# Gate and up projections as one 2x2x2 block product with seven products, over half-token columns, and FFN pools laid over the attention's

## The chip, the cores and the metric

The kernel runs on one core of a Trainium2 chip. The metric is the device time of one execution in microseconds (us); lower is better. Three executions of the kernel before took 701.97, 702.12 and 705.43 us, median 702.12. A core has TensorE (PE, matrix products into PSUM), VectorE (DVE), ScalarE (ACT), GpSimd (POOL, which works on SBUF only), SyncE (SP, which issues the loads here) and DMA engines. Each engine takes its instructions in order and waits on semaphores for the others.

## The reference

One residual block of an encoder: attention (two groups of heads), a convolutional FFN, and a gated per-layer embedding. 512 tokens, model width 1024, FFN width 2816. The part that matters here:

```
x  = x + concat(mla_heads, diff_heads) @ w_out
h2 = rmsnorm(x) * ffn_norm_g
g  = h2 @ w_gate                      # 1024 -> 2816
c  = conv_b + sum_j shift(g, 2 - j) * conv_w[j]     # causal, width 3
x  = x + (silu(c) * (h2 @ w_up)) @ w_down
x  = x + sigmoid(rmsnorm(x) @ w_pg) * (p @ w_pp)
```

Everything is float32 in the inputs and the output.

## The kernel before

All activations are kept transposed: features on the 128 partitions, the 512 tokens along the free axis. x is eight blocks of [128, 512] (`xb(b)`). A product of float32 numbers is made as three products of rounded halves (`mm3`, lines 151 to 156): each operand is split into hi (rounded by a ScalarE copy, L188 or L147) and lo (the remainder, by a VectorE subtraction, L189, L192 or L148), and PE adds hi*hi, hi*lo and lo*hi into one PSUM bank. The norm's per-token factor is applied after the products, since it commutes with them; the gain of the norm is folded into the split of x.

The FFN runs over f = 0 to 21, each a block of 128 of the 2816 columns (`gu_full`, L782). For each f, `gu_w` loads two weight tiles [128, 8 x 128] from w_gate and w_up and splits them; `gu_mm` makes the gate and the up product, each 8 blocks of the contraction x 3 matmuls with 512 token columns, into a bank each (g, u). `gu_post` (L768) multiplies the gate by the norm's factor nr (VectorE, L772), runs the three-tap convolution (ScalarE L773, VectorE L774 and L775) and silu (ScalarE L776), multiplies by the factor (GpSimd, L777) and by the up bank (VectorE, L778), and splits the result into `ah[f]`, `al[f]`. After every `DOWN_GROUPS` = (6, 6, 6, 4) blocks of f comes the down projection of that group: for each of the eight output blocks b, 3 x nf matmuls of 512 columns (`down`, L794) and an addition to x on VectorE (L575). The halves dh of w_down are loaded as tiles of two f by four b.

Before the FFN, `wo_last` finishes the output projection block by block, each followed by `norm_in` (L736): the split of the block with the gain, its square on ScalarE, and the sum of squares on VectorE or GpSimd (L745). `norm_r` (L747) sums over partitions with a matmul of ones and computes the reciprocal root on tiles of [128, 512]. After the FFN the last down group is followed in the same way by `norm_in` for the embedding stage, which multiplies with w_pg and w_pp (`ple`, L849). Its last block runs as two halves of 256 columns.

The order of PE's instructions is that of the program text; the other engines' queues are ordered by a planner that goes by priorities and its own costs. All tiles lie in one SBUF pool for the whole kernel, with rotating buffers by tag (raw 3, hi and lo 5, th and tl 8, tt 16). PSUM has eight banks: acc 2, lg 3, tp 2, ob 1.

Of the kernel before, what the change touches and what calls it, by code (L numbers as in the profile page):

```python
# [20 lines left out]
P = 128  # L21
T = 512
NT = 4
# [12 lines left out]
# columns of the packed per-partition array  # L36
# [15 lines left out]
DOWN_GROUPS = (6, 6, 6, 4)  # L52
# [3 lines left out]
# units of filling work at the attention's steps  # L56
# [7 lines left out]
# which of VectorE (0) and GpSimdE (1) does a step, by tiles  # L64
# [35 lines left out]
def hybrid_block(ctx: ExitStack, tc: tile.TileContext, a: dict, out: bass.AP):  # L100
# [12 lines left out]
    def tt(name, dtype=F32):  # L113
        return sb.tile([P, T], dtype, tag="tt", bufs=16, name=name)

    def sq_tile(name):
        return sb.tile([P, D], F32, tag="sq", bufs=2, name=name)

    def pm_tile(name):
        return sb.tile([P, T], F32, tag="pm", bufs=PM, name=name)  # L120

    def pt_tile(name):
        return sb.tile([P, T], F32, tag="pt", bufs=2, name=name)

    def xn_tile(name):
        return sb.tile([P, D], F32, tag="xn", bufs=4, name=name)

    def kv_tile(name, dtype=F32):
        return sb.tile([P, NT, H, 160], dtype, tag="kv", name=name)

    def th_tile(name):
        return sb.tile([P, T], F32R, tag="th", bufs=8, name=name), sb.tile([P, T], F32R, tag="tl", bufs=8, name=name + "l")

    def small(name, shape):
        return sb.tile(shape, F32, name=name)

    def load_raw(src, n, name):
        raw = sb.tile([P, 1024], F32, tag="raw", bufs=3, name=f"raw_{name}")
# [3 lines left out]
    def load_w(src, n, name, eng=None):  # L142
        """a tile of weights as hi + lo"""
        raw = load_raw(src, n, name)
        hi = sb.tile([P, 1024], F32R, tag="hi", bufs=NW, name=f"hi_{name}")
        lo = sb.tile([P, 1024], F32R, tag="lo", bufs=NW, name=f"lo_{name}")
# [4 lines left out]
    def mm3(ps, blocks, first=True, last=True):  # L151
        n = len(blocks)
        for i, (xh, xl, wh, wl) in enumerate(blocks):
            TE.matmul(ps, xh, wh, start=first and i == 0, stop=False)  # L154
            TE.matmul(ps, xh, wl, start=False, stop=False)  # L155
            TE.matmul(ps, xl, wh, start=False, stop=last and i == n - 1)  # L156
# [28 lines left out]
    def split(h_, l_, src, col=None, eng=None):  # L185
        """hi and lo of src, times a gain for each partition"""
# [9 lines left out]
    # the tensor engine's clock and the activation tables get ready while the first loads run  # L196
    ones, warm = small("ones", [P, P]), small("warm", [P, 1])
# [11 lines left out]
    def squares(kq):  # L209
        """squares of x, for the sums over its columns"""  # L210
# [7 lines left out]
    cols = small("cols", [P, NCOL])  # L218
    nc.sync.dma_start(cols, a["cols"])
    xh, xl, wa = [], [], []  # L220
    for kq in range(4):
        raw = xn_tile(f"xT{kq}")
        xraw.append(raw)
        wr = sb.tile([P, 1024], F32, tag="raw", bufs=3, name=f"raw_a{kq}")
        wh, wl = (sb.tile([P, 1024], F32R, tag=i, bufs=NW, name=f"{i}_a{kq}") for i in ("hi", "lo"))
# [21 lines left out]
    ident = small("ident", [P, P])  # L247
# [20 lines left out]
    # latents: normalise  # L268
# [19 lines left out]
    # weights of the up-projections  # L288
# [64 lines left out]
    st_ = sb.tile([P, NK, T], F32R, tag="st", name="st")  # L353
# [11 lines left out]
    # rope tables with the gains folded in: [c g1 | c g2], [-s g2 | s g1]  # L365
# [16 lines left out]
    # rope of the shared key  # L382
# [11 lines left out]
    # gains of the MLA heads: those of k's nope part go to q's side, with the scale  # L394
# [3 lines left out]
    # differential heads: both gains and minus the scale on q's side  # L398
# [55 lines left out]
    # -lambda on every partition  # L454
# [21 lines left out]
    def probs_T(pm, t, name, on_act):  # L476
        """transposed probabilities of a tile of queries"""
# [59 lines left out]
    def bias_strip():  # L537
        """minus the relative position bias as a strip for each head, S[p, h, j] = -f_h(j - 384 - p)"""
# [9 lines left out]
        strip = sb.tile([P, DH, T], F32, tag="strip", name="strip")  # L548
# [16 lines left out]
    def wo_blocks(k0, k1, b, w):  # L565
        """blocks k0..k1 of the contraction of w_out with the mixer's output, for a block of x^T"""
# [3 lines left out]
    def xb(b):  # L570
        """a block of x^T"""
# [10 lines left out]
    def wo_units(kq, dqs, nk):  # L582
        """the product with the first nk blocks of a half of w_out's rows, added to x^T"""
# [366 lines left out]
```

## Time and profile before

| | |
|---|---|
| Median of three runs | 702.12 us |
| Profiled execution | span 706.7 us; no other time is given for it |
| PE busy | 677.1 us, 3242 matmuls |
| VectorE busy | 424.2 us, 754 instructions |
| ScalarE busy | 288.4 us |
| GpSimd busy | 139.0 us |
| DMA | 63.38 MB, mean 90 GB/s |

Engines overlap, so the busy times do not add up to the span. A matmul's row shows its latency, with an end that is modelled; the rate is read from the distance between starts. A row of instructions gives the start, the duration, the engine, the line, the operation, the output tile and its inputs, and in brackets how long the engine had been idle and what released it. Line numbers are those of the kernel before.

### The profile page before, as it was taken

The numbers are of one execution on the slowest core, as the hardware profiler recorded it, in microseconds if no ns is written. First come the engines' busy times: TensorE is split into PE (matmuls) and PEld (weight loads), VectorE is DVE, ScalarE is ACT, GpSimd is POOL, SyncE is SP. The second block draws the span as 40 slices with busy tenths as digits, with TensorE's granted clock in tenths as the row PEclk, the third lists the DMA queues.
The fourth block names the chain that finished last, engine by engine and source line by source line (L and its number), as shares of the span: only waits on it lengthen the run. The fifth ranks groups of instructions, "written<-read, shape, count | busy, mean of one in ns | idle before, by whom it ended". The sixth has DMA issues, their size and how long they took to land.

```text
span 706.7 us, 8596 instructions
## 1 busy us (share of the span) xinstructions
PE 677.1 (96%) x3242; PEld 554.8 (79%) x3242; DVE 424.2 (60%) x754; ACT 288.4 (41%) x500; POOL 139.0 (20%) x136
## 2 busy tenths in 40 slices
PE   7988889999999997999999999999999999999997
PEld 6877678788878785788888888888888888877886
DVE  6689964634779878774544545534554455468743
ACT  6156645536666654343421333312333233255210
POOL 6458341504010125021100011100101000132000
PEclk9899999999999998999999999999999999999999
DMA  7332014303311103233213333222233132243101
GB/s 261 106 121 89 30 60 135 120 1 111 129 30 61 31 31 105 74 99 110 90 42 108 119 102 106 90 90 89 90 103 103 63 119 90 89 150 104 60 31 45
DMA packets 19552, 63.38 MB, mean 90 GB/s; under 512 B 2220, under 2 KB 2988, under 8 KB 19384
## 3 DMA queue, kind: packets, MB, share of 16 engines
q1 hardware_dynamic: 18776, 60.25, 25.9%
q0 software_dynamic: 448, 2.37, 1.1%
q8 instruction: 25, 0.41, 0.2%
q10 hardware_dynamic: 288, 0.23, 0.1%
q14 instruction: 15, 0.12, 0.1%
HBM read 60.73 MB, written 3.42 MB: 91 GB/s over the span
## 4 chain that ended last, share of the span: by engine, by line
PE 76%; DVE 14%; ACT 3%; issue 2%; POOL 2%; DMA 2%; SPq 0%; ACTq 0%; DVEq 0%; POOLq 0%
PE u L154 6%; PE u L156 6%; PE u L155 6%; PE g L156 6%; PE g L155 6%; PE g L154 6%; PE dn L154 5%; PE dn L155 5%; PE dn L156 5%; PE pg L154 2%; PE pg L156 2%; PE pg L155 2%; PE mo L527 2%; PE zd L154 2%; PE zd L156 2%
## 5 line engine op out<-in xcount | busy, mean ns | idle before, releaser
L777 POOL TENSOR_TENSOR cv<-cv,nr 128x512 f32<-128x512 f32 x22 | 28.7, 1308 | 297.9 <-ACT cv L776 297.9
L155 PE MATMUL g<-h2l,hi_g 128*128 128x512 f32 x176 | 69.6, 396 | 4.7 <-DVE h2l L192 4.7
L154 PE MATMUL dn<-ah,hi_dn 128*128 128x512 f32 x176 | 69.8, 397 | 2.1 <-DVE x L575 2.1
L154 PE MATMUL u<-h2h,hi_u 128*128 128x512 f32 x176 | 70.5, 401 | 0.0
L154 PE MATMUL g<-h2h,hi_g 128*128 128x512 f32 x176 | 70.4, 400 | 0.0
L156 PE MATMUL u<-h2h,lo_u 128*128 128x512 f32 x176 | 70.2, 399 | 0.0
L156 PE MATMUL g<-h2h,lo_g 128*128 128x512 f32 x176 | 70.0, 398 | 0.0
L155 PE MATMUL u<-h2l,hi_u 128*128 128x512 f32 x176 | 69.6, 396 | 0.0
L156 PE MATMUL dn<-ah,lo_dn 128*128 128x512 f32 x176 | 69.5, 395 | 0.0
L575 DVE TENSOR_TENSOR x<-x,dn 128x512 f32<-128x512 f32 x32 | 21.9, 685 | 51.1 <-PE dn L156 51.1
L147 ACT CAST hi_dn<-raw_dn 128x1024 fp32r<-128x1024 f32 x22 | 23.1, 1051 | 69.3 <-PE dn L155 29.7
L772 DVE TENSOR_TENSOR gr<-g,nr 128x512 f32<-128x512 f32 x22 | 15.1, 691 | 53.7 <-PE g L156 53.6
L147 ACT CAST hi_g<-raw_g 128x1024 fp32r<-128x1024 f32 x22 | 23.0, 1047 | 57.9 <-PE dn L155 39.9
L147 ACT CAST hi_u<-raw_u 128x1024 fp32r<-128x1024 f32 x22 | 23.1, 1052 | 55.4 <-PE g L155 50.0
L155 PEld LDWEIGHTS g<-h2l,hi_g 128*128 128x128 f32 x176 | 33.3, 189 | 13.9 <-DVE h2l L192 5.9
L778 DVE TENSOR_TENSOR cv<-cv,u 128x512 f32<-128x512 f32 x22 | 15.1, 688 | 44.4 <-POOL cv L777 44.4
L154 PEld LDWEIGHTS dn<-ah,hi_dn 128*128 128x128 f32 x176 | 33.0, 187 | 10.8 <-DVE x L575 1.9
L154 PE MATMUL zd<-hi_d,xh 128*128 128x512 f32 x96 | 40.2, 418 | 0.0
L156 PEld LDWEIGHTS u<-h2h,lo_u 128*128 128x128 f32 x176 | 33.5, 190 | 8.4
L155 PEld LDWEIGHTS u<-h2l,hi_u 128*128 128x128 f32 x176 | 33.5, 190 | 8.2
L156 PEld LDWEIGHTS g<-h2h,lo_g 128*128 128x128 f32 x176 | 33.3, 189 | 8.1
L154 PEld LDWEIGHTS u<-h2h,hi_u 128*128 128x128 f32 x176 | 33.6, 191 | 7.7
(371 smaller groups left out, 1657.4 us busy)
## 6 DMA issues: line engine op xcount, KB each, us to landing
raw_g<-in_w_gate SPq DMA_DIRECT2D x22, 512.0 KB, 3.6
raw_u<-in_w_up SPq DMA_DIRECT2D x22, 512.0 KB, 3.5
raw_dn<-in_w_down SPq DMA_DIRECT2D x22, 512.0 KB, 3.5
raw_d<-in_w_d SPq DMA_DIRECT2D x12, 512.0 KB, 3.7
raw_o<-in_w_out SPq DMA_DIRECT2D x8, 512.0 KB, 4.0
raw_pg<-in_w_pg SPq DMA_DIRECT2D x8, 512.0 KB, 3.6
x<-in_xT SPq DMA_DIRECT2D x4, 512.0 KB, 5.6
out<-ot SPq DMA_DIRECT2D x7, 256.0 KB, 2.0
```

Source lines behind the costliest of these rows:

```text
L147: S.copy(hi[:, :n], raw[:, :n])
L154: TE.matmul(ps, xh, wh, start=first and i == 0, stop=False)
L155: TE.matmul(ps, xh, wl, start=False, stop=False)
L156: TE.matmul(ps, xl, wh, start=False, stop=last and i == n - 1)
L527: TE.matmul(po[:, w], pt[:, tsl[j]], kv[j][:, h, 96:], start=j == 0, stop=j == t)
L575: V.tensor_tensor(xb(b), xb(b), ps, op=ALU.add)
L772: V.tensor_tensor(gr, pg_, nrm["r"], op=ALU.mult)
L777: G.tensor_tensor(cv, cv, nrm["r"], op=ALU.mult)
L778: V.tensor_tensor(cv, cv, pu, op=ALU.mult)
```

## The change

Gate and up of one f are written as one product of 2x2 blocks: the weights' two halves of the contraction by (gate, up), and x's two halves of the contraction by the two halves of the tokens (256 columns each). Four quadrants of the result (gate and up, first and second half of the tokens) come from seven products, each of 4 contraction blocks x 3 matmuls with 256 columns, in place of the eight of plain blocks. Operands of these products are sums and differences of quadrants.

- `w_prep(f)` loads the two weight tiles, forms the four weight sums (two on GpSimd, two on VectorE, 512 wide each) and splits four tiles (three of 1024, one of 512) into hi and lo.
- `tokens(k)`, for k = 0 to 3, forms from x blocks k and k + 4 the token quadrants and four sums on GpSimd (256 wide each), and splits them.
- `gu_units(f)` is a generator of seven units. PSUM banks are used again without clearing: x collects P1, then P1 + S2 T2, then also S3 T3; y collects S1 T1, then also S4 b22. ScalarE copies x out three times, VectorE combines to the four quadrants.
- `gu_post` multiplies gate and up by the norm's factor in one VectorE operation of 1024; the GpSimd multiplication is gone.
- `norm_r` sums squares to [128, 4] with tokens on the partitions, takes the root there, and `norm_b` spreads the factor with a diagonal matrix and a matmul of ones. All square sums are on VectorE.
- `DOWN_GROUPS` is (4, 4, 4, 4, 6). The down products of the first four groups are units of a filling queue, two of them in each f from 5 to 20; the last group follows f = 21.
- The last blocks of the output projection run in the order 0, 4, 1, 5, 2, 6, 3, 7.
- There are pools of their own for attention (`att`, `wts`), FFN (`ffn`, `dwn`) and embedding (`ple`), a later one laid over an earlier one, where a new tile waits for the old tiles that it lies over. Raw weight tiles have 4 buffers in the FFN, hi and lo of the down weights 2.

```
-DOWN_GROUPS = (6, 6, 6, 4)
+DOWN_GROUPS = (4, 4, 4, 4, 6)
...
-    sb = ctx.enter_context(tc.tile_pool(name="sb", bufs=1))
+    keep = ctx.enter_context(tc.tile_pool(name="keep", bufs=1))
+    att = tc.alloc_tile_pool(name="att", bufs=1, side="left")
+    wts = tc.alloc_tile_pool(name="wts", bufs=1, side="right")
...
+    order = (0, 4, 1, 5, 2, 6, 3, 7)
...
+    att.release()
+    wts.release()
+    ffn = tc.alloc_tile_pool(name="ffn", bufs=1, side="left", reuse_waits="tile")
+    dwn = tc.alloc_tile_pool(name="dwn", bufs=1, side="right", reuse_waits="tile")
+    wp.update(pool=dwn, rawpool=ffn, raw=4, w=2)
...
+    def w_prep(f):
+        ra, rb = (load_raw(a[w][f], 1024, f"{w[2]}{f}") for w in ("w_gate", "w_up"))
+        sa, sb = (ffn.tile([P, 1024], F32, tag=i, name=f"{i}{f}") for i in ("sa", "sb"))
+        l, r = slice(0, 512), slice(512, 1024)
+        G.tensor_tensor(sa[:, r], rb[:, l], rb[:, r], op=ALU.add)
+        V.tensor_tensor(sa[:, l], sa[:, r], ra[:, l], op=ALU.subtract)
+        G.tensor_tensor(sb[:, l], ra[:, l], rb[:, l], op=ALU.subtract)
+        V.tensor_tensor(sb[:, r], ra[:, r], sa[:, l], op=ALU.subtract)
+        w = {}
+        for i, (src, n, keys) in enumerate(((ra, 1024, ("11", "12")), (sa, 1024, ("S2", "S1")), (sb, 1024, ("S3", "S4")), (rb[:, r], 512, ("22",)))):
+            h_, l_ = (ffn.tile([P, n], F32R, tag=f"{j}{i}", bufs=2 if i == 0 else 1, name=f"{j}{i}_{f}") for j in ("wh", "wl"))
+            split(h_, l_, src)
...
+    def tokens(k):
+        gu = ffn.tile([P, 2, T], F32, tag="gu", bufs=2, name="xg")
+        for j in range(2):
+            S.activation(gu[:, j], xb(k + K2 * j), AF.Identity, scale=cols[:, C_FFN + k + K2 * j:C_FFN + k + K2 * j + 1])
+        split(b11[0][:, k], b11[1][:, k], gu[:, 0, t1])
+        split(b2[0][:, k], b2[1][:, k], gu[:, 1])
+        ts_ = ffn.tile([P, 4, H2], F32, tag="s", bufs=2, name="ts")
+        G.tensor_tensor(ts_[:, 0], gu[:, 0, t2], gu[:, 0, t1], op=ALU.subtract)
+        G.tensor_tensor(ts_[:, 1], gu[:, 1, t2], ts_[:, 0], op=ALU.subtract)
+        G.tensor_tensor(ts_[:, 2], gu[:, 1, t2], gu[:, 0, t2], op=ALU.subtract)
+        G.tensor_tensor(ts_[:, 3], ts_[:, 1], gu[:, 1, t1], op=ALU.subtract)
+        split(bt[0][:, k], bt[1][:, k], ts_)
...
+    def product(ps, w, b, more=False):
+        mm3(ps, [(w[0][:, tsl_k[k]], w[1][:, tsl_k[k]], b[0][:, k], b[1][:, k]) for k in range(K2)], not more, True, more)
...
+    def gu_units(f, w):
+        x = bank("acc", f"gx{f}")[:, :H2]
...
+        product(x, w["11"], tb["11"])
+        S.copy(s[:, 0], x)
+        yield
+        p2 = bank("tp", f"ga{f}")[:, :H2]
+        product(p2, w["12"], tb["21"])
+        V.tensor_tensor(gu[:, 0, t1], s[:, 0], p2, op=ALU.add)
+        yield
+        product(x, w["S2"], tb[2], True)
+        S.copy(s[:, 1], x)
+        yield
+        y = bank("lg", f"gb{f}")[:, :H2]
+        product(y, w["S1"], tb[1])
+        yield
+        p4 = bank("tp", f"gc{f}")[:, :H2]
+        product(p4, w["22"], tb[4])
+        yield
+        product(x, w["S3"], tb[3], True)
+        S.copy(s[:, 2], x)
+        V.tensor_tensor(gu[:, 1, t1], s[:, 2], p4, op=ALU.subtract)
+        V.tensor_tensor(gu[:, 1, t2], s[:, 2], y, op=ALU.add)
+        yield
+        product(y, w["S4"], tb["22"], True)
+        V.tensor_tensor(gu[:, 0, t2], s[:, 1], y, op=ALU.add)
+        gu_post(f, gu)
+        yield
...
     def gu_post(f, gu):
...
-        V.tensor_tensor(gr, pg_, nrm["r"], op=ALU.mult)
+        V.tensor_tensor(gu, gu, nrm["r"].unsqueeze(1).broadcast_to([P, 2, T]), op=ALU.mult)
...
-        G.tensor_tensor(cv, cv, nrm["r"], op=ALU.mult)
-        V.tensor_tensor(cv, cv, pu, op=ALU.mult)
+        V.tensor_tensor(cv, cv, up, op=ALU.mult)
...
+    w = {0: w_prep(0)}
+    for k in range(K2):
+        tokens(k)
+        for b in (k, k + K2):
+            square(b, dwn)
+    g = gu_units(0, w[0])
+    next(g)
+    next(g)
+    for f in range(NF):
+        if f + 1 < NF:
+            w[f + 1] = w_prep(f + 1)
+            g1 = gu_units(f + 1, w[f + 1])
+        if f == 0:
+            next(g1)
+            next(g1)
+            norm_r()
+            next(g)
+            norm_b(ffn)
+        else:
+            next(g)
+        for _ in range(3):
+            next(g)
+        if f and f + 1 < NF:
+            next(g1)
+        if f:
+            pump()
+        for _ in g:
+            pass
+        if f and f + 1 < NF:
+            next(g1)
+            pump()
+        for f0, nf in groups[:-1]:
+            if f == f0 + nf:
+                fill.append(down_units(f0, nf))
+        g = g1
+    pump(100)
```

So within one f from 1 on, PE's order is: products S2, S1, 22, S3 of f, product 11 of f + 1, a down unit, product S4 of f, product 12 of f + 1, a down unit.

More of the change, by code (lines that the diff above doesn't have):

```diff
@@ L741, in norm_in, with square @@
+    def square(b, pool):
+        if "ss" not in nrm:
+            nrm["ss"] = pool.tile([P, T], F32, tag="ah", bufs=8, name="ss")
             S.activation(nrm["ss"], xb(b), AF.Square)
         else:
-            sq = pt_tile("nsq")
+            sq = pool.tile([P, T], F32, tag="al", bufs=8, name="nsq")
             S.activation(sq, xb(b), AF.Square)
-            (G if b % 2 else V).tensor_tensor(nrm["ss"], nrm["ss"], sq, op=ALU.add)
+            V.tensor_tensor(nrm["ss"], nrm["ss"], sq, op=ALU.add)
@@ L747, in norm_r @@
     def norm_r():
-        ps = bank("ob", "nr")
-        TE.matmul(ps, ones, nrm["ss"], start=True, stop=True)
-        r, m, g, t = (w_[:, i] for w_ in [sb.tile([P, DH, T], F32, tag="strip", name="nr")] for i in range(4))
-        rms(r, ps, T, D, m, (g, t))
-        return r
-    h2h = sb.tile([P, NK, T], F32R, tag="st", name="h2h")
-    h2l = kv_tile("h2l", F32R).rearrange("p t h d -> p (t h d)")[:, :NK * T].rearrange("p (k t) -> p k t", t=T)
+        ss, ps = nrm.pop("ss"), bank("ob", "nr")
@@ new lines, in hybrid_block, with load_w3, norm_in @@
+    pump(100)
+    ffn.release()
+    ple_ = tc.alloc_tile_pool(name="ple", bufs=1, side="left", reuse_waits="tile")
+    def load_w3(src, name):
+        raw = ple_.tile([P, 1024], F32, tag="raw", bufs=3, name=f"raw_{name}")
+        nc.sync.dma_start(raw, src)
+        h_, l_ = (ple_.tile([P, 1024], F32R, tag=i, bufs=NW, name=f"{i}_{name}") for i in ("hi", "lo"))
+        split(h_, l_, raw)
+        return h_, l_
+    def norm_in(b, hh, hl_, c):
+        split(hh[:, b], hl_[:, b], xb(b), cols[:, c + b:c + b + 1])
+        square(b, dwn)
@@ L874, in hybrid_block @@
     ple(NK - 1, w, 256, 512)
+    ple_.release()
+    dwn.release()
 def _constants():
```

172 lines of the change are left out of this document (88 added, 84 removed).

## The prediction

> **What bounds the kernel now.** I read the page's busy shares first, then the busy time by stage, then single instructions of the stage that the change rebuilds.
>
> ```profile
> span 706.7 us, 8596 instructions
> PE 677.1 (96%) x3242; PEld 554.8 (79%) x3242; DVE 424.2 (60%) x754; ACT 288.4 (41%) x500; POOL 139.0 (20%) x136
> ```
>
> ```profile
> 257.00:285.00 28.00, 23.33 (x89) 18.16 (x88) 22.71 (x21) 14.69 (x22) 14.32 (x7) 0.88 0.29 94
> 285.00:360.00 75.00, 75.00 (x323) 60.16 (x322) 46.90 (x60) 28.34 (x35) 9.33 (x7) 1.00 0.30 92
> 360.00:640.00 280.00, 277.94 (x1194) 223.56 (x1192) 137.82 (x160) 89.64 (x110) 28.29 (x21) 1.00 0.30 98
> ```
>
> The columns of the second view are the stretch, PE, PE weight loads, VectorE, ScalarE, GpSimd, granted clock, DMA. TensorE (PE) is the bound: in the FFN's 360 to 640 us it is busy 277.94 of 280, at full clock, while VectorE works 137.82, about half. Only the entry of the FFN, 257 to 285, is not PE's: there VectorE is busy 22.71 of 28 and the granted clock falls to 0.88. Busy PE time hides overlap, so I take the step from one matmul to the next:
>
> ```profile
> 330.42 0.40 PE L154 MATMUL g<-h2h,hi_g 128*128 128x512 f32 x1
> ...
> 335.77 0.40 PE L156 MATMUL g<-h2h,lo_g 128*128 128x512 f32 x1
> ```
>
> ```profile
> 698.83 0.29 PE L154 MATMUL pg<-h3h,hi_pg 128*128 128x256 f32 x1
> ...
> 701.54 0.28 PE L156 MATMUL pg<-h3h,lo_pg 128*128 128x256 f32 x1
> 701.55 0.19 PEld L154 LDWEIGHTS pp<-pt,pp 128*128 128x128 f32 x1
> ```
>
> The first pair brackets 24 matmuls of 512 columns: 5.35/23 = 0.2326 us each. The second brackets 24 of 256 columns, each with a weight load of its own: 2.71/23 = 0.1178 us. So half the columns cost half the time.
>
> **TensorE's part of the change.** Gate and up for one f (128 FFN columns) were 2 x 8 x 3 = 48 matmuls of 512: 48 x 0.2326 = 11.16 us. Seven products of 4 x 3 matmuls of 256 are 84 x 0.1178 = 9.90. That removes 1.27 us per f, 27.9 us over 22. The down projection keeps its 528 matmuls (24 x 0.2326 = 5.58 us per f), in groups (4,4,4,4,6): of the first four, 32 units of 12 matmuls, two in each of f = 5 to 20; the last group grows from 8 x 12 to 8 x 18 matmuls.
>
> [...] The 0.1178 us step, with a load in every step, says the load is hidden; the measured step decides.
>
> **VectorE's part.** Its prices, from back-to-back rows:
>
> ```profile
> 405.22 0.75 DVE L774 SCALAR_TENSOR_TENSOR cv<-gr,cols,cv 128x511 f32<-128x511 f32 x1
> 406.00 0.75 DVE L775 SCALAR_TENSOR_TENSOR cv<-gr,cols,cv 128x510 f32<-128x510 f32 x1
> ...
> 409.66 1.23 DVE L148 TENSOR_TENSOR lo_g<-raw_g,hi_g 128x1024 fp32r<-128x1024 f32 x1
> 410.80 0.69 DVE L189 TENSOR_TENSOR al<-cv,ah 128x512 fp32r<-128x512 f32 x1
> ...
> 606.82 0.69 DVE L189 TENSOR_TENSOR pt0l<-raw_p,pt 128x512 fp32r<-128x512 f32 x1
> 607.42 0.69 DVE L189 TENSOR_TENSOR pt1l<-raw_p,pt 128x512 fp32r<-128x512 f32 x1
> ...
> 698.32 0.42 DVE L862 TENSOR_TENSOR sg<-pg,nr 128x256 f32<-128x256 f32 x1 [1.35 <-PE pg L156]
> ```
>
> A 1024-wide operation occupies 1.14 us, a 512-wide one 0.60, a scalar_tensor_tensor 0.78; a 256-wide one lasts 0.42, less the same 0.09 of overlap 0.33. Per f the new kernel has on VectorE: two of the weights' sums, 1.20; low halves of three 1024-wide and one 512-wide tile, 4.02; four 256-wide combinations of PSUM, 1.32; the post step (1024-wide multiply by the norm, two scalar_tensor_tensors, two 512-wide) 3.90. Together 10.44. From f = 5 on, a down weight (1.14) and two adds to x (1.20) make it 12.78. The old kernel's list at the same prices (three 1024-wide, three 512-wide, two scalar_tensor_tensors, 8/6 of an add) is 7.6 us beside 16.7 of PE. New: 10.44 beside 9.90 for f = 0 to 4, and 12.78 beside 15.48 later.
>
> **GpSimd's part, and what it does to VectorE.** Per f GpSimd gives up one 512-wide multiply and gets two 512-wide sums:
>
> ```profile
> L777 POOL TENSOR_TENSOR cv<-cv,nr 128x512 f32<-128x512 f32 x22 | 28.7, 1308 | 297.9 <-ACT cv L776 297.9
> L426 POOL TENSOR_TENSOR qn<-rt 128x256 f32<-128x256 f32 x4 | 3.0, 747 | 3.3 <-DVE rs_t L172 2.6 <-DVE rt L425 0.3 <-POOL rt L423 0.3
> ```
>
> That is 2.6 us per f. The old multiply ran while VectorE waited for it anyway; the new sums run beside a loaded VectorE. What that costs shows in the old FFN's entry (two views, VectorE and GpSimd):
>
> ```profile
> 267.58 2.89 DVE L745 TENSOR_TENSOR ss<-ss,nsq 128x512 f32<-128x512 f32 x1
> 270.40 0.67 DVE L575 TENSOR_TENSOR x<-x,o 128x512 f32<-128x512 f32 x1
> ...
> 272.95 2.26 DVE L192 SCALAR_TENSOR_TENSOR h2l<-x,cols,h2h 128x512 fp32r<-128x512 f32 x1
> ```
>
> ```profile
> 267.07 2.85 POOL L148 TENSOR_TENSOR lo_g<-raw_g,hi_g 128x1024 fp32r<-128x1024 f32 x1
> 270.62 1.26 POOL L745 TENSOR_TENSOR ss<-ss,nsq 128x512 f32<-128x512 f32 x1 [0.69 <-DVE ss L745]
> 271.84 2.83 POOL L148 TENSOR_TENSOR lo_u<-raw_u,hi_u 128x1024 fp32r<-128x1024 f32 x1
> ```
>
> VectorE's 0.69 us add took 2.89 and ended at 270.47, 0.55 after GpSimd's operation ended at 269.92; the scalar_tensor_tensor took 2.26 and ended 0.54 after GpSimd's. A VectorE operation with two SBUF inputs waits the GpSimd operation out. The add to x, with one input in PSUM, took 0.67 under GpSimd as always. So GpSimd's time is added to VectorE's wherever it meets two-SBUF work: 9.12 of the 10.44 us (87%), which gives 10.44 + 0.87 x 2.6 = 12.7 for f = 0 to 4; later 10.26 us of such work in a 15.48 us period (66%), 12.78 + 1.7 = 14.5. The ends are 10.4 and 13.0, 12.8 and 15.4. I take 12.5 for f = 0 to 4: VectorE is the bound there by 2.6 us per f. For f = 5 to 20 it is loaded to 94% of PE's period, in a queue kept in order, with operations that wait for ScalarE and PE; I take 16.0 us, between PE's 15.48 and 17.0 (12.78 + 2.6 + some 1.6 of waits, two STT prices).
>
> **The entry of the FFN.** The old one lost this on PE:
>
> ```profile
> 272.49 0.51 PE L155 MATMUL g<-h2l,hi_g 128*128 128x512 f32 x1 [2.85 <-DVE h2l L192]
> ...
> 275.27 0.80 PE L155 MATMUL g<-h2l,hi_g 128*128 128x512 f32 x1 [1.82 <-DVE h2l L192]
> 275.86 0.63 PE L156 MATMUL g<-h2h,lo_g 128*128 128x512 f32 x1
> ...
> 281.41 0.41 PE L154 MATMUL u<-h2h,hi_u 128*128 128x512 f32 x1
> ```
>
> Idle 4.67, and 13 steps at 0.427 instead of 0.2326, 2.5: 7.2 us. The new kernel first makes the token operands, for each of four pairs of blocks: on VectorE splits of 256, 512 and 1024 (0.33 + 0.60 + 1.14) and two square sums (1.20; the squares that GpSimd added are VectorE's now), 3.27; on GpSimd four 256-wide sums at 0.75, 3.0. Times four, 13.1 + 12.0 = 25.1, nearly all of it two-SBUF work, so one after the other. The two engines also prepare weights for f = 0 (5.22 + 2.6); their raw tiles lie over attention tiles that the last head's norm still reads shortly before the entry, so I put half of that, 3.9, behind.
>
> ```profile
> 257.12 2.73 DVE L575 TENSOR_TENSOR x<-x,o 128x512 f32<-128x512 f32 x4 [1.27 <-PE o L156]
> ```
>
> The adds to x start at 257.12 and take 0.68; after the first pair of them and two 512-wide gains on ScalarE, token work starts near 260. Operands of all seven products are ready at 260 + 25.1 + 3.9, some 288 (282 if weights are early and GpSimd's sums slip under the adds; 293 with all weights behind). PE meanwhile has four products for f = 0 and 1, 5.65 us, and then waits. Reordering the output projection keeps its matmuls; its adds to x merely arrive in pairs. The norm's four-wide rsqrt replaces 512-wide steps, which PE's queue hid; with its diagonal it costs VectorE about as much as the part of f = 1's weights that fits in the waits saves: nothing.
>
> **New waits.** S4 adds onto the bank of S1, so PE waits for one ScalarE copy and two VectorE steps after S3, all 256-wide; behind it queue the next f's product and a down unit. For f above 4 a product and a unit of 2.8 us lie between: hidden. At f = 21 nothing does: 1.3 us (three steps of 0.42) to 1.7 with the signals between. ScalarE was busy 89.64 of 280 us, 5.4 per f; even with twice that it would not be the bound. Down weights have two buffers: casts for the next half wait for the last unit, with five products (7.1 us) as cover and 2.3 us of VectorE work in it; that is in the 16.0. DMA counts are unchanged (66 FFN tiles of 512 KB).
>
> The last group now follows f = 21 at once; before, four units of 18 matmuls lay between. Its weights lie over token operands that S4 reads last: a load (3.5, the row below), cast, low half (1.14) come after it, while f = 21's post step ends; the first 12 matmuls cover 2.8. I take 6 us, bounds 3 and 9.
>
> ```profile
> raw_dn<-in_w_down SPq DMA_DIRECT2D x22, 512.0 KB, 3.5
> ```
>
> The embedding stage's first matmul follows its last one:
>
> ```profile
> 645.70 0.40 PE L154 MATMUL pg<-h3h,hi_pg 128*128 128x512 f32 x1
> ```
>
> **The sum**, in the profile's time: 288 + 5 x 12.5 - 3.9 (the post step of f = 4 runs under f = 5) = 346.6; + 16 x 16.0 = 602.6; f = 21, five products and the stall, 7.1 + 1.7 = 611.4; + 6 = 617.4; + 144 x 0.2326 = 650.9; the embedding stage as before, 706.7 - 645.7 = 61.0: 711.9. That is 5.2 above the old span of 706.7. The span is the only time shown for that execution; it lies 4.6 above the runs' median of 702.12 and 1.3 above the highest run, so I carry the difference over: **707 us**. The 27.9 us saved on PE go: some 10 at the entry, some 12 in f = 0 to 4, 8 in f = 5 to 20, 4 at the tail beyond what was lost there before.
>
> **Rivals.** *VectorE keeps up.* GpSimd's sums fall into VectorE's waits and under PSUM operations: operands at 284, 11.0 per f, then PE's own 15.48, a 4 us tail: 284 + 55 - 3.9 + 247.7 + 8.8 + 4 + 33.5 + 61 = 690, 17 less than before: 686 us. For it: the demand, 14.5, is under 15.48, and most dependences have several microseconds of slack. Against: f = 0 to 4 stay above PE even at 10.44. It decides if VectorE's share in f = 5 to 20 stays under about 95% with PE dense.
>
> *VectorE is the bound all along.* At 17.0 us per f from f = 5 on, 16 more: 723 us. For it: 15.4 without any overlap, plus waits for activations in a fixed order; against: the schedule has other work to put in.
>
> *Weight loads show.* If a 256-column step cost a load's 0.188 us (its row above, 0.19), PE would need 15.8 per f, 22 x 4.6 = 102 more than before, about 804. The 0.1178 steps speak against it; what is new is only that they go on for long.
>
> **Chances.** Forecast 0.46 (699 to 717), VectorE keeps up 0.33 (679 to 698), VectorE bound 0.19 (717 to 735), weight loads 0.02. Half a per cent, 3.5 us, is what this measurement tells from no change. Of the forecast's 0.46, 0.18 lie within it and 0.28 above. So faster 0.33, same 0.18, slower 0.28 + 0.19 + 0.02 = 0.49. All low ends together give 679, all high ends 734; I take 682 to 727.
>
> **What would show it.** The 256-column step: 0.118, else the fourth case. VectorE's busy share above 95% for f = 1 to 4 and PE idle there some 2.5 us per f, released by VectorE; VectorE rows of 1.2 us stretched past 2 where GpSimd runs. PE's period for f = 5 to 20: 15.5 means the first rival, 17 the second. First S2 product near 288; an idle of some 6 us on PE before the last group. I am wrong if PE is dense from 300 on, or if the operands are ready before 280.

## The result, and the profile after

The changed kernel takes 737.83 us (median of 4 runs, 735.52 to 740.57) beside 703.7 for the kernel before in the same comparison: ratio 1.0482, 95% interval 1.0437 to 1.0527. It is 4.8% slower; the prediction was 707, with a range of 682 to 727. The page of the changed kernel, and its busy time by stage in the columns of the prediction's second view:

```profile
span 738.8 us, 10590 instructions
PE 665.8 (90%) x4050; PEld 589.0 (80%) x4050; DVE 549.0 (74%) x956; ACT 351.6 (48%) x624; POOL 178.2 (24%) x162
```

```profile
257.00:285.00 28.00, 10.38 (x40) 7.61 (x38) 22.80 (x22) 14.44 (x23) 17.63 (x14) 0.72 0.11 38
285.00:360.00 75.00, 54.82 (x381) 52.27 (x382) 57.33 (x84) 35.32 (x53) 18.48 (x15) 0.85 0.19 57
360.00:640.00 280.00, 266.91 (x1858) 250.04 (x1856) 236.79 (x316) 131.31 (x195) 54.15 (x33) 0.98 0.30 93
```

TensorE worked 23.33 of 28 us and all of the next 75 before; now 10.38 and 54.82, at granted clocks of 0.72 and 0.85. In the last row PE is short by 13 us, most of it at the end. So PE lacks work at the entry, less so up to f=5, and at the tail, and not in between.

**The entry.** ScalarE, TensorE, VectorE and GpSimd rows of the changed kernel:

```profile
264.27 1.33 ACT L780 ACTIVATE xg<-x,cols 128x512 f32<-128x512 f32 x2 [9.38 <-PE o L160]
```

```profile
293.34 0.58 PE L160 MATMUL gx<-b11l,wh 128*128 128x256 f32 x1 [2.31 <-DVE b11l L194]
...
298.88 0.38 PE L161 MATMUL gx<-b11h,wl 128*128 128x256 f32 x1 [1.64 <-DVE wl L194]
...
303.93 0.36 PE L159 MATMUL gx<-bth,wh 128*128 128x256 f32 x1
```

```profile
276.46 1.21 DVE L798 TENSOR_TENSOR ss<-ss,nsq 128x512 f32<-128x512 f32 x1
...
295.55 1.21 DVE L194 TENSOR_TENSOR btl<-ts,bth 128x1024 fp32r<-128x1024 f32 x1
```

```profile
275.95 1.17 POOL L787 TENSOR_TENSOR ts<-ts,xg 128x256 f32<-128x256 f32 x1
...
278.88 2.18 POOL L759 TENSOR_TENSOR sa<-raw_u 128x512 f32<-128x512 f32 x1 [1.76 <-DVE wl L194]
```

ScalarE sat 9.38 us before the first token operand and was released by an output-projection matmul, though the adds to x had begun at 256.96. Then VectorE and GpSimd work against each other until GpSimd ends at 293.87: the 512-wide VectorE operation shown takes 1.21 (0.69 alone), a 256-wide GpSimd one 1.17 (0.75 alone), a 512-wide one 2.18 (1.31). The last VectorE row is the last token operand, ready at 296.76; at 1024 columns 1.21 is its ordinary duration. TensorE finishes the first product at 293.9, waits again for f=1's weights, and begins S2 of f=0 at 303.93.

**f=1 to 4.** S4 of f=0 and of f=4 on TensorE, 51.7 us apart, 12.9 per f; then that stretch by engines, and what VectorE and, from 300 to 372, TensorE waited for (us in total, times, longest):

```profile
315.78 0.39 PE L159 MATMUL gb<-b2h,wh 128*128 128x256 f32 x1 [2.51 <-DVE gu L851]
...
367.49 0.39 PE L159 MATMUL gb<-b2h,wh 128*128 128x256 f32 x1 [2.19 <-DVE gu L851]
```

```profile
315.50:367.50 52.00, 42.77 (x325) 41.96 (x325) 43.09 (x58) 27.47 (x41) 13.03 (x8) 0.93 0.25 76
```

```profile
DVE gu L854 <- PE gb L161: 5.5, 4, 2.0
DVE sa L760 <- POOL sa L759: 2.2, 3, 1.2
```

```profile
PE gb L159 <- DVE gu L851: 11.5, 5, 2.5
```

VectorE is busy 83%, not full: it waits for S4 (gu L854 needs bank gb) and for GpSimd's sum, while TensorE waits for VectorE before S4. They wait in turn. For TensorE the period of 12.9 is 84 steps of 0.120 (10.1), 2.2 of wait and some 0.6 of slower steps: its granted clock in that stretch is 0.93, and 0.52 from 316.90 to 320.40, behind the first of these waits.

**f=5 to 20, and the tail.** The middle of the FFN, then S4 of f=21, the last group, and ScalarE's queue between them:

```profile
375.00:623.00 248.00, 246.62 (x1707) 230.37 (x1706) 213.58 (x285) 116.75 (x171) 49.31 (x30) 1.00 0.31 94
```

```profile
622.85 0.28 PE L159 MATMUL gx<-bth,wh 128*128 128x256 f32 x1
...
623.81 0.28 PE L161 MATMUL gx<-bth,wl 128*128 128x256 f32 x1
...
630.02 0.39 PE L159 MATMUL gb<-b2h,wh 128*128 128x256 f32 x1 [1.25 <-DVE gu L851]
...
639.99 0.80 PE L159 MATMUL dn<-ah,hi_dn 128*128 128x512 f32 x1 [8.28 <-ACT hi_dn L193]
...
642.27 0.63 PE L160 MATMUL dn<-al,hi_dn 128*128 128x512 f32 x1
642.70 0.63 PE L161 MATMUL dn<-ah,lo_dn 128*128 128x512 f32 x1
```

```profile
633.47 0.81 ACT L864 ACTIVATE cv<-gu,cols 128x512 f32<-128x512 f32 x1 [4.29 <-DVE gu L863]
...
638.90 1.99 ACT L193 CAST hi_dn<-raw_dn 128x1024 fp32r<-128x1024 f32 x2
```

In the middle PE is dense (246.62 of 248) at full clock with VectorE at 86%, and a 256-column matmul with its weight load takes 0.96/8 = 0.120 us. Behind S4 of f=21 nothing covers its post step: the cast of the last group's weights stands behind the activations of f=21 in ScalarE's queue, PE idles 8.28 us and starts the last group with steps of 0.43 us, about twice the usual (granted clock 0.53 from 640 to 645).

### The profile page after: what moved, and what is told of

Same layout as the page of the kernel before. It is cut to its first block, busy times and chain, and to the rows that moved or that the text cites. A ratio compares the mean times of both kernels' runs of the same rounds, so it can differ in the third digit from the quotient of the medians.

```text
span 738.8 us, 10590 instructions
## 1 busy us (share of the span) xinstructions
PE 665.8 (90%) x4050; PEld 589.0 (80%) x4050; DVE 549.0 (74%) x956; ACT 351.6 (48%) x624; POOL 178.2 (24%) x162
## 4 chain that ended last, share of the span: by engine, by line
PE 59%; DVE 20%; issue 8%; POOL 5%; ACT 4%; DMA 3%; SPq 0%; POOLq 0%; ACTq 0%; DVEq 0%
PE dn L161 5%; PE dn L159 5%; PE dn L160 5%; PE gx L159 3%; PE gx L160 3%; PE gx L161 3%; DVE wl L194 2%; PE gb L159 2%; PE gb L161 2%; PE gb L160 2%; PE mo L532 2%; PE pg L161 2%; PE pg L160 2%; PE pg L159 2%; PE zd L159 2%
## 5 line engine op out<-in xcount | busy, mean ns | idle before, releaser
L759 POOL TENSOR_TENSOR sa<-raw_u 128x512 f32<-128x512 f32 x22 | 39.7, 1805 | 140.8 <-DMA raw_u<-in_w_up 65.2
L160 PE MATMUL dn<-al,hi_dn 128*128 128x512 f32 x176 | 69.6, 396 | 0.0
L761 POOL TENSOR_TENSOR sb<-raw_g,raw_u 128x512 f32<-128x512 f32 x22 | 33.6, 1528 | 110.1 <-DVE wl L194 110.1
L159 PE MATMUL gx<-bth,wh 128*128 128x256 f32 x176 | 50.6, 287 | 0.7 <-ACT s L840 0.6
L160 PE MATMUL gx<-btl,wh 128*128 128x256 f32 x176 | 50.3, 286 | 0.0
L161 PE MATMUL gx<-bth,wl 128*128 128x256 f32 x176 | 50.3, 286 | 0.0
L160 PE MATMUL zd<-lo_d,xh 128*128 128x512 f32 x96 | 38.1, 396 | 0.0
L159 PEld LDWEIGHTS gx<-bth,wh 128*128 128x128 f32 x176 | 34.2, 195 | 1.8 <-ACT s L840 1.1
L160 PEld LDWEIGHTS gx<-btl,wh 128*128 128x128 f32 x176 | 34.3, 195 | 0.7
L161 PEld LDWEIGHTS gx<-bth,wl 128*128 128x128 f32 x176 | 34.3, 195 | 0.0
## 6 DMA issues: line engine op xcount, KB each, us to landing
out<-ot SPq DMA_DIRECT2D x7, 256.0 KB, 2.0
```

Source lines behind the costliest of these rows:

```text
L159: TE.matmul(ps, xh, wh, start=first and i == 0, stop=False, skip_group_check=again)
L160: TE.matmul(ps, xh, wl, start=False, stop=False, skip_group_check=again)
L161: TE.matmul(ps, xl, wh, start=False, stop=last and i == n - 1, skip_group_check=again)
L759: G.tensor_tensor(sa[:, r], rb[:, l], rb[:, r], op=ALU.add)
L761: G.tensor_tensor(sb[:, l], ra[:, l], rb[:, l], op=ALU.subtract)
```

## Experiments

All ratios are to the kernel before, run on the same chip; the changed kernel's is 1.0482. Savings in us are differences of such ratios times 704. In profiled executions the FFN's beginning differs by 1 to 3 us, so stages are compared from a row near it.

**Where the first scratch lies.**

```diff
+    early_t = {0: (ffn.tile([P, 2, T], F32, tag="gu", bufs=2, name="xg"), ffn.tile([P, 4, H2], F32, tag="s", bufs=2, name="ts"))}
     b11, b2, bt = hl("b11", [P, K2, H2]), hl("b2", [P, K2, T]), hl("bt", [P, K2, 4, H2])
...
-        gu = ffn.tile([P, 2, T], F32, tag="gu", bufs=2, name="xg")
+        gu, ts_ = early_t.pop(k) if k in early_t else (ffn.tile([P, 2, T], F32, tag="gu", bufs=2, name="xg"), None)
```

> Only the place of the scratch of the first token pair is changed: xg and its sums lie over attention tiles that are free early, not over the w_out weights that the last output-projection matmul reads. If the place of the scratch is what delays the entry, ScalarE's first xg row comes before 260 us and no longer behind an o matmul, the product S2 of f=0 starts near 298 instead of 303.9, and the time falls by about 6 us, to some 732. If the 25 us of serial VectorE and GpSimd work sets the entry by itself, whatever it waits for at the start, the start moves by as much all the same: 4 to 6 us. If the weights of f=0 set the end of the entry (the product 11 waits for b11 of the last pair, which stands behind them in ScalarE's and VectorE's queues), the first xg comes earlier and S2 does not: under 2 us.

735.5 us, ratio 1.0414 (1.0377 to 1.0452). ScalarE's first row there:

```profile
254.66 1.40 ACT L781 ACTIVATE xg<-x,cols 128x512 f32<-128x512 f32 x2 [2.80 <-DVE x L580]
```

The wait for the o matmul is gone, xg follows x at once. S2 of f=0 came at 296.16; with 3.0 us by which this execution was early already at ScalarE's last yh row (251.16 against 254.20), that is 4.7 earlier. The ratios differ by 0.0068, 4.8 us. Their intervals just overlap (1.0437 against 1.0452), but the profile shows the same 4.7: the place of the scratch costs about 5 us.

**GpSimd's sums on VectorE.** All six lines of this kind:

```diff
-        G.tensor_tensor(sa[:, r], rb[:, l], rb[:, r], op=ALU.add)
+        V.tensor_tensor(sa[:, r], rb[:, l], rb[:, r], op=ALU.add)
```

> All sums that GpSimd made (two per f of the weights, four per pair of the tokens) are on VectorE instead; the results are the same. By the lock (a VectorE operation with two SBUF inputs waits out a GpSimd operation) GpSimd's time is VectorE's time already, at GpSimd's dearer price (0.75 against about 0.33 us for 256 columns, 1.3 against 0.6 for 512): the entry's 25.1 us become 13.1 + 16 x 0.33 = 18.4, S2 of f=0 comes some 6 us earlier, f=1 to 4 cost at most what they did (12.9 us each), and the time falls by 5 to 9 us. By the rival, that GpSimd really works beside VectorE, VectorE gets 1.2 us more per f and 5.3 us more at the entry: f=1 to 4 take about 14 us each, f=5 to 20 rise from 15.7 to above 16, and the time rises by 5 us or more.

727.69 us, ratio 1.0306 (1.0276 to 1.0336): 12.4 us less, more than either end of the expectation. VectorE in f=1 to 4, and its two convolution lines (us in total, mean ns), here and then in the changed kernel:

```profile
310.00:356.00 46.00, 41.31 (x336) 40.50 (x337) 44.57 (x66) 28.58 (x41) 0.00 (x0) 1.00 0.32 100
```

```profile
L865 DVE SCALAR_TENSOR_TENSOR cv<-gu,cols,cv 128x511 f32<-128x511 f32 x22 | 16.4, 748 | 0.9 <-ACT cv L864 0.9
L866 DVE SCALAR_TENSOR_TENSOR cv<-gu,cols,cv 128x510 f32<-128x510 f32 x22 | 16.4, 744 | 0.0
```

```profile
L865 DVE SCALAR_TENSOR_TENSOR cv<-gu,cols,cv 128x511 f32<-128x511 f32 x22 | 25.6, 1164 | 1.9 <-ACT cv L864 1.7
L866 DVE SCALAR_TENSOR_TENSOR cv<-gu,cols,cv 128x510 f32<-128x510 f32 x22 | 22.7, 1030 | 0.0
...
L760 DVE TENSOR_TENSOR sa<-sa,raw_g 128x512 f32<-128x512 f32 x20 | 13.8, 692 | 21.4 <-POOL sa L759 21.4
```

VectorE did 60 operations more and its busy time rose by only 5.1 us (549.0 to 554.1): 44 of 0.60 and 16 of 0.33 are 31.7 us, so some 27 us of stretch went, and 21.4 us of waiting for GpSimd's sum besides. Stretch and waiting together were more than the 31.7 us of the work itself. Now VectorE is full in f=1 to 4, 97%. S4 of f=0 and of f=4 begin at

```profile
309.86 0.39 PE L159 MATMUL gb<-b2h,wh 128*128 128x256 f32 x1 [1.25 <-DVE gu L851]
...
354.46 0.39 PE L159 MATMUL gb<-b2h,wh 128*128 128x256 f32 x1 [1.28 <-DVE gu L851]
```

That is 11.15 us per f, and 11.6 in the last two of the four; 10.44 plus the two sums at 0.60 is 11.64. How the two engines meet shows in the changed kernel's trace: GpSimd's 512-wide sum at 269.77 lasted 2.28 (1.31 alone), to 272.05, beside a VectorE split that ended at 270.92, and the next VectorE split, 1024 wide, at 270.84, lasted 2.29 (1.21 alone), to 273.13. So each ended 1.1 us after the one before it on the other engine.

**S4 later.**

```diff
+            next(g1)
             for _ in g:    # S4 of f
                 pass
-            next(g1)
```

> Only the order on TensorE changes, for f=1 to 20: the second product of f+1 (12) runs before S4 of f instead of behind it, which puts 2.8 us instead of 1.4 between S3 and S4 where there is no down unit. If f=1 to 4 are slow because S4 waits for a chain of short steps on ScalarE and VectorE (2.0 to 2.5 us of TensorE idle each), they fall from 12.9 to 11 to 11.5 us and the total by 5 to 8 us. If VectorE's throughput with GpSimd's locks is the bound there, as predicted, the wait appears elsewhere: 12.5 us or more each, total within 2 us. For f=5 to 20 no change either way.

734.71 us, ratio 1.0402 (1.0378 to 1.0426), 5.6 less. What VectorE waited for in this kernel's f=1 to 4:

```profile
314.00:364.40 50.40, 42.75 (x336) 41.94 (x336) 45.80 (x56) 26.53 (x40) 13.35 (x8) 0.97 0.28 84
```

```profile
DVE gu L854 <- PE gb L161: 2.6, 2, 1.8
DVE sa L760 <- POOL sa L759: 1.2, 1, 1.2
```

Neither theory: the period fell only to 12.6, PE still waited about 2 us before most S4, and VectorE's share rose from 83 to 91%. VectorE's wait for S4 was one part of the loop; with it shortened VectorE is nearer its limit. Between S2 of f=0 and S2 of f=5 the trace accounts for 3 of the 5.6 us (65.0 against 68.0); some 1.5 lie ahead of S2 of f=0, where nothing was changed.

**The seven products undone.**

```diff
-        product(x, w["11"], tb["11"])
...
+        product(pg_, w["11"], b1)
...
+        product(pg_, w["12"], b2, True)
...
```

Six more of the seven products go, and the bank of up, pu, gets the same two lines.

> The changed kernel without the seven products: gate and up as four plain block products of 512 columns (48 matmuls), no sums of weights or tokens, no combinations; the pools over the attention's, the four-wide norm, the order of the f and the down groups (4,4,4,4,6) stay; the result is the same function. If the seven products (their operands, combinations and locks) cost the time, this goes to between 698 and 712: TensorE needs 11.16 us per f where it took 12.9 in f=1 to 4, and 16.7 per f for f=5 to 20 against 15.7 (16 us worse), while the entry is at least 15 us shorter. If the pools, the norm and the new tail cost it, it stays above 725, with f=0 to 4 at 11.2 and the entry and tail as late as in the changed kernel.

707.58 us, ratio 1.0025 (1.0003 to 1.0047). So pools, norm and groups cost 0.25%, the seven products, with the operands that they need, the other 4.6. Up's first product of f=8 and that of f=10 begin there, and product 22 of f=12 and f=14 in the changed kernel, at

```profile
383.44 0.39 PE L159 MATMUL gb<-b1h,wh 128*128 128x512 f32 x1
...
416.34 0.39 PE L159 MATMUL gb<-b1h,wh 128*128 128x512 f32 x1
```

```profile
484.55 0.28 PE L159 MATMUL gc<-bth,wh 128*128 128x256 f32 x1
...
515.64 0.28 PE L159 MATMUL gc<-bth,wh 128*128 128x256 f32 x1
```

That is 32.90/2 = 16.45 us per f against 31.09/2 = 15.55: where PE is dense, the seven products gain 0.90 us per f. In f=1 to 4, without down units, it is the other way round: there the plain kernel takes 10.88 us per f (the same product begins at 290.58 for f=1 and at 334.10 for f=5) where the changed one takes 12.9.

**The tail's cover.**

```diff
-DOWN_GROUPS = (4, 4, 4, 4, 6)
+DOWN_GROUPS = (2, 4, 4, 4, 4, 4)
```

> Only the down projection's groups change: (2, 4, 4, 4, 4, 4) instead of (4, 4, 4, 4, 6), so that four units of 12 matmuls are left when f=21 is reached, one between its S3 and S4 and three (8.4 us) behind S4, and the last group has 12 matmuls per block instead of 18. If the gap before the last group is want of cover, the 8.28 us and the steps at half clock behind it (some 2.5 us) go, f=3 and 4 pay 1 to 2 us each for adds that come earlier, and the time falls by 8 to 10 us, to some 729. If the last group's weights themselves come late (they lie over token operands that S4 of f=21 reads), the gap stays at 3 to 5 us behind the three units and the time falls by 4 us or less.

728.24 us, ratio 1.0330 (1.0300 to 1.0359), 10.7 less. TensorE behind f=21 in that kernel:

```profile
636.23 0.50 PE L159 MATMUL dn<-ah,hi_dn 128*128 128x512 f32 x1 [0.59 <-ACT hi_dn L193]
...
638.76 0.50 PE L161 MATMUL dn<-ah,lo_dn 128*128 128x512 f32 x1 [1.80 <-DVE lo_dn L194]
```

The 8.28 became 0.59 and 1.80, though some eight steps of 0.43 remain: want of cover, as the first theory had it. Not all of the saving lies there. S4 of f=21 began at 625.88 instead of 630.02, though a unit now stands ahead of it: the first group's small units ran in TensorE's waits, and from S4 of f=2 to S4 of f=4 it took 26.1 us with three of them and 26.3 without. The expectation's 1 to 2 us of cost in f=3 and in f=4 did not come.

**All repairs, and TensorE's order at the entry.** First the three repairs together:

> The three repairs together, seven products for every f: the first scratch laid where it is free early, all sums on VectorE, the groups (2, 4, 4, 4, 4, 4). Alone they gave 4.8 and 12.4 us, the third is estimated at 8 to 10. If the losses are separate, 709 to 716; then what is left over the kernel before is the entry, where the products wait for 18 us of operand work whatever its order, and the change cannot be faster without another entry. If they share a cause, 718 or more. Below 704 the entry would not be a loss of its own.

720.18 us, ratio 1.0216 (1.0185 to 1.0246). Alone the three took off 0.0068, 0.0176 and 0.0152, together 0.0266 instead of 0.0396: they draw on the same slack. From S4 of f=0 to S4 of f=4 it takes 47.95 us against 44.60 with the sums alone: the first down units now lie on a full VectorE (46.18 of 47.95 us busy). TensorE's last wait at the entry is as long as with the sums alone:

```profile
292.90 0.58 PE L161 MATMUL gx<-b11h,wl 128*128 128x256 f32 x1 [5.91 <-DVE wl L194]
```

This is f=1's first product, which stands ahead of S2 of f=0. Two runs put f=1's products behind f=0's, and the norm behind S1 of f=0, in the changed kernel and in the repaired one:

```diff
         if f == 0:
-            next(g1)      # products 11 and 12 of f=1
-            next(g1)
-            norm_r()
+        for i in range(4):
             next(g)
...
+            if f == 0 and i == 1:
+                norm_r()
...
```

> Against the changed kernel only TensorE's order at the entry changes: the products 11 and 12 of f=1 run behind the products of f=0 as for every later f, and the norm's matmuls behind S1 of f=0. In the changed kernel bt was finished at 296.8 and S2 of f=0 began at 303.93, behind the two products of f=1 at half clock and the norm. If that order costs the entry, S2 of f=0 comes at 297 and the time falls by 4 to 7 us. If VectorE's serial work sets the entry whatever TensorE's order (f=1's weights are then late by as much), the first product of f=1 waits instead and the time changes by less than 2 us.

> The three repairs (scratch, sums on VectorE, groups) and this order, seven products for every f. In the run with the sums on VectorE, VectorE had the last operands at 289.9 and worked without a gap from 263.4 to 294.0, but TensorE waited 5.91 us to 292.92 for the first product of f=1, which stands before S2 of f=0. If the order is what is left, S2 of f=0 begins at 290 and the time falls from 720 by 5 to 8 us, to 712 to 715: still above the kernel before. If VectorE's work is the floor, 718 to 720.

735.27 us, ratio 1.0434 (1.0400 to 1.0468), and 720.01, ratio 1.0202 (1.0174 to 1.0230). The first interval overlaps the changed kernel's, the second is the repaired kernel's again. In the former S2 came at 293.09, and the wait came back at the norm:

```profile
304.53 2.05 PE L813 MATMUL nrb<-dg,ones 128*128 128x512 f32 x2 [5.67 <-DVE dg L808]
```

VectorE's queue there shows what the norm waited for:

```profile
297.37 0.16 DVE L184 TENSOR_SCALAR rs_m<-nr 128x4 f32<-128x4 f32 x1 [1.95 <-PE nr L804]
297.45 1.23 DVE L194 TENSOR_TENSOR wl<-raw_g,wh 128x1024 fp32r<-128x1024 f32 x1
...
301.56 0.69 DVE L760 TENSOR_TENSOR sa<-sa,raw_g 128x512 f32<-128x512 f32 x1
302.17 0.15 DVE L175 TENSOR_TENSOR rs_g<-r,rs_m 128x4 f32<-128x4 f32 x1
```

Between the first step of the norm and the one at 302.17 stand three splits and a sum of weights, and one more step of the norm at 300.33. So TensorE's order is not what is left; what TensorE waits for is VectorE's queue. Whether the amount of work in it or its order costs the time was not tested with seven products.

**Plain products first, seven products where down units run beside them.**

```diff
+NPL = 5
...
+    for f in range(NPL):
+        w[f + 1] = w_prep(f + 1)
...
+    for f in range(NPL, NF):
```

The first loop makes plain products and the token sums of one pair of blocks per f; the second is the changed kernel's, with all sums on VectorE.

> f=0 to 4, which have no down units beside them, as plain block products (the same function), f=5 to 21 as seven products; the four token sums are made one pair of blocks per f in f=0 to 3, all sums on VectorE; groups as in the changed kernel. If the loss lies at the entry and in f=0 to 4, where VectorE is the bound, and the seven products gain where down units lie beside them, the time is the plain kernel's 707.6 less 16 x 1.15 (16.7 against 15.55 us) plus some 5 at the tail: 690 to 696. If making the operands costs its 10 us of VectorE wherever it is put, 700 to 705; if the 15.55 needs the late start that the changed kernel had (weights ahead of time), above 705.

The second of these two runs has the tail's groups as well, and the token sums in f=0 to 2:

> The same, with the down groups (2, 4, 4, 4, 4, 4) and the token sums in f=0 to 2. If cover is what the tail wants, 8 us less than the former: 682 to 688, faster than the kernel before by some 2.5 per cent. If VectorE cannot take the first units' adds in f=3 and 4 beside the rest, the same as the former within 3 us.

704.14 us, ratio 0.9983 (0.9966 to 0.9999), and 698.72, ratio 0.9912 (0.9881 to 0.9942): right in sign, 8 and 11 us short of what was expected. In both, gate and up of f=0 to 4 lack the first weight block's product for the first 256 tokens (the last section says why); every matmul runs all the same. f=5 to 20 went at 15.55 with whole units beside them; what seemed to be missing was the entry, where an operand lay over the last w_out weights again (ScalarE waited 6.2 us there). The next run moves it, and begins each plain product with its 512 columns, so that nothing is lost:

```diff
-    b12 = [tuple(dwn.tile([P, 2, H2], F32R, tag="a" + j, bufs=8, name=f"b12{j}{i}") for j in "hl") for i in range(K2 // 2)]
+    b12 = [ffn.tile([P, K2, H2], F32R, tag="s", bufs=2, name="b12" + j) for j in "hl"]
...
-            b1_product(pp[f, i], w[f][f"{i + 1}1"])
+            product(pp[f, i], w[f][f"{i + 1}2"], b2)
```

> As hybrid_tail (plain products for f=0 to 4, seven products from f=5 on, sums on VectorE, groups (2, 4, 4, 4, 4, 4)), with two differences. The second half of the token operands of the plain products lies in scratch that the seven products do not use yet, over attention tiles that are free early, instead of over the last w_out weights: there ScalarE idled 6.25 us for an o matmul, and the first gate matmul came at 268.05. And each plain product begins with the 512-column half, onto which both 256-column halves are added, so that no term is lost: hybrid and hybrid_tail began each half of a bank by itself and lose the product of the first weight and token blocks for the first 256 tokens in f=0 to 4. If the place of the operands was what was left at the entry, the first gate matmul comes at 263 to 264, and the time falls from 698.7 by 4 to 7 us, to 692 to 695. If VectorE's queue sets the entry, it stays within 2 us of 698.

698.89 us, ratio 0.9890 (0.9864 to 0.9916): the second theory, although the first gate matmul did come at 263.29 instead of 268.05. TensorE now waited for VectorE instead (us in total, times, longest):

```profile
PE gx L161 <- DVE b2l L198: 4.3, 3, 2.0
PE gx L162 <- DVE wl L195: 2.5, 1, 2.5
```

The last run gives the entry's work another order:

```diff
     for k in range(K2):
         tokens(k)
+    for k in range(K2):
+        tokens1(k)
+    for k in range(K2):
         for b in (k, k + K2):
             square(b, ffn, "cv")
...
-            product(pp[f, i], w[f][f"{i + 1}2"], b2)
+            (wh_, wl_), n = w[f][f"{i + 1}2"], 3 * K2
...
```

`tokens` now makes the operand of 512 columns alone and `tokens1` the two of 256, and the squares come last. The first product of a weight block makes the eight matmuls with the weights' high half ahead of the four with the low half.

> As hybrid2, with the entry's work put in the order in which TensorE asks for it: the token operands of the 512-column half first, then the two 256-column halves, the squares of the norm last, and in the first product of a weight block all matmuls with the weights' high half ahead of those with the low half. In hybrid2 TensorE waited four times at the entry, 6.8 us in all, and ran at half clock until 279. If VectorE's order there is the cause, the waits shrink to 2 or 3 us, full clock comes at about 273, and the time is 4 to 6 us below hybrid2's 698.9. If the amount of VectorE's work behind the last add to x sets it, less than 2 us.

691.33 us (6 runs, 689.73 to 693.93), ratio **0.9793** (0.9763 to 0.9822), 0.0097 or 6.8 us less than hybrid2. Its entry, and the one wait of its products there:

```profile
257.00:285.00 28.00, 24.02 (x125) 20.33 (x124) 22.41 (x39) 16.48 (x26) 0.00 (x0) 0.94 0.49 147
```

```profile
269.59 0.50 PE L853 MATMUL gx<-b2h,wh 128*128 128x512 f32 x1 [3.67 <-ACT wh L194]
```

PE works 24.02 of the 28 us, at clock 0.94; VectorE's busy time there is as large as ever (22.41), only the order has changed. The first theory: 6.8 us where 4 to 6 were expected. The order of VectorE's work and that of the matmuls in a product changed together and were not run apart. This version is 2.1% faster than the kernel before. By the periods its 17 f with seven products gain 17 x 0.90, some 15 us; what its groups and its order at the entry would give with plain products throughout was not run.

## Why the prediction was wrong

In profile time, the prediction's checkpoints against the trace (S2 of f=5 and f=21 for "f=5 starts" and "f=21"):

| stage | predicted | measured | difference |
|---|---|---|---|
| operands ready / S2 of f=0 | 288 | 303.93 | +15.9 |
| f=0 to 4 | 58.6 | 68.0 (to 371.97) | +9.4 |
| f=5 to 20 | 256.0 | 250.9 (to 622.85) | -5.1 |
| f=21 and gap before the last group | 14.8 | 17.1 (to 639.99) | +2.3 |
| last group | 33.5 | 36.3 (to 676.32) | +2.8 |
| embedding stage, to the end | 61.0 | 62.5 (to 738.8) | +1.5 |

- **The step of a matmul: right, the saving mis-sized.** 0.120 us per 256 columns with a weight load in each step, so "weight loads show" fell: the rows of those loads show 0.195 us on average, more than the whole step. But the saving was 0.90 us per f, not 1.27: the two bracketed pairs gave 0.2326 and 0.1178, the periods of 16.45 and 15.55 give less between them. Most of the difference is the 512-column step, which is 16.45/72 = 0.2285 where PE is dense.
- **The entry: the step that failed most.** "Token work starts near 260": it started at 264.27, since the prediction left out what the new scratch lies on; the run with the scratch moved shows that wait gone. "25.1 + 3.9": it took 32.5 us from 264.27 to 296.76, not 28 from 260 (the terms add up to 289.0, which the sum takes as 288), with all of f=0's weights in it and not half, and f=1's four sums as well. That GpSimd's and VectorE's work add up there was right in kind (the sums on VectorE shorten it). "PE meanwhile has four products and then waits": the first of the four waits for its operands one after the other, the third for f=1's weights, and three of the four run mostly at steps of 0.21 (granted clock 0.55 from 293 to 297, 0.62 from 299 to 303); with the norm, 7.2 us passed from the last operand to S2. Of the 15.9 us, then, 4.3 are the later start, 4.5 the longer operand work and 7.2 what came behind it. "The norm: nothing" was wrong too, but taking order and norm out of S2's way did not bring the time back: TensorE then waited 5.67 us at the norm, for VectorE's queue. How much of this is the amount of VectorE's work and how much its order stays open.
- **f=0 to 4: the size nearly right, the reason half.** 12.5 predicted, 12.9 measured. That is 2.1 of the 9.4; the rest is the 3.9 that I took off for the last post step, which a sum of PE periods already contains, and the remaining 3.4, about what TensorE lost for the norm in f=0 (305.45 to 308.8). I named VectorE's throughput with GpSimd's time added; VectorE was busy only 83%. S4's wait, which I considered for f=21 alone, GpSimd's sum that VectorE waited for, and the stretch come together in the 12.9; the runs with the sums moved and with S4 later each shortened a part, but the parts were not separated fully. That 12.5 came so near is in part luck. Throughput is the bound only once the sums are moved, and then at 11.15, with 11.6 in the last two periods, as the list of operations gives (11.64).
- **f=5 to 20: too dear.** 15.68 per f instead of 16.0. Here "VectorE keeps up" was right by its own test: VectorE at 86%, PE dense. It gave 686 because it took the entry to be as cheap.
- **f=21 and the tail: inside the bounds, at the dear end.** The S4 wait was 1.25 (1.3 to 1.7 predicted); the gap 8.28 where I took 6 of 3 to 9. I left out that the last group begins at about half clock, steps of 0.43 up to 644.4: most of its +2.8. The run with the groups changed shows that the gap is want of cover.

The sum of 711.9 thus missed the span by 26.9 us, 25.3 of it at the entry and in f=0 to 4: the stages that I had worked out as engine sums, without what starts them, what PE's clock does meanwhile, and what stands in each queue. The other 3.9 us up to the measured 737.83 are no stage: the prediction took off 4.9 from profile time to its 707, and here the median lies only 1.0 below the span.

## What to carry to other kernels

A change that trades matmul columns for vector work gains where the vector engine has slack in that very stage: here in f=5 to 20, beside down units (15.55 us per f against 16.45 with plain products), and not in f=1 to 4 (12.9 against 10.88); done there alone, with the sums on VectorE, cover at the tail and another order at the entry, it went from 4.8% slower to 2.1% faster. Before an entry is costed, look up on which tiles the first scratch of a new pool lies and who reads them last, and what in each engine's queue stands ahead of the first product. Small sums given to GpSimd to relieve VectorE can cost VectorE more than doing them: here some 27 us of stretch and 21.4 of waiting against 31.7 of work.

## What was not expected of the hardware

- Moving 90 us of GpSimd work onto VectorE raised VectorE's busy time by 5.1 us and made the kernel 12.4 us faster. The stretch falls on either engine: at 512 columns GpSimd's two sums took 1.81 and 1.53 us on average over the changed kernel's 22 f, where 1.31 was the old kernel's price, and VectorE's two convolution lines 1.16 and 1.03, where they took 0.75 and 0.74 with those sums on VectorE.
- A start reached beyond its own columns. In hybrid and hybrid_tail each 256-column half of a bank began with a start of its own, and a 512-column product was then added to both. Their output differs from the reference by 0.05125 of its norm, and the reference computed without the first weight block's product for the first 256 tokens in f=0 to 4 differs by 0.05125 as well. So what the first half had collected before the second start is missing from its sum.
